# Strassen projection products: two blocks of 272 columns against one block of 512 with the samples' 64 columns beside them

## The chip, the cores and the metric

One core of a Trainium2 chip runs the whole kernel as a single program. The metric is the device time of one execution in microseconds, and the median over several executions is compared. TensorE (PE in the profile; its weight loads are shown as PEld) multiplies, VectorE (DVE), ScalarE (ACT) and GpSimd (POOL) do the elementwise work, and the queues of SyncE (SP) and ScalarE issue most transfers between the chip's memory and the core.

## The reference, cut to what matters

One layer of a hybrid decoder runs over a prompt of 1024 rows and over 8 samples of 8 rows, with all numbers in float32. After an RMSNorm and a modulation, one wide projection feeds everything else:

```
h = rmsnorm(x) * (1 + scale) + shift
[u_pool | z_pool | z_ssm | xBC | dt | g] = h @ w_in        # 1024 -> 8224 columns
p = (pool_mix(u_pool) * silu(z_pool)) @ w_pool_out
s = gated_rmsnorm(SSD(conv(xBC)) + D*x, z_ssm) @ w_ssm_out
x = x + gate * ((sigmoid(g_pool) * p + sigmoid(g_ssm) * s) @ w_o)
```

The outputs are the two normed results and the new pool, conv and SSM states of the prompt and of the samples. This case is about `h @ w_in`, and about the step that carries the samples' SSM states through their 8 rows.

## The kernel before, in words

The kernel keeps activations transposed: 128 channels lie on the partitions, and the T = 1088 columns are the 1024 prompt rows followed by the 64 sample rows. Every float32 operand of a large product is split into a high part (rounded to the fast float32r type) and a low part (the rest), and a product is the sum of three float32r products: high by high, high by low, low by high. In `product` these are three matmuls for each of four blocks of 128 channels, so 12 matmuls make one sum in a PSUM bank.

**The projection.** After `first` (start-up, norm, modulation, and two blocks of 128 output channels by plain products) 62 blocks of 128 output channels of `w_in` are left. They are made two at a time by `pair`, 31 pairs, each with the Strassen-Winograd scheme of seven products: the four 512x128 weight blocks b11, b12, b21, b22 of a pair are combined by `pair_w` (a few differences, then `split` into `whi` and `wlo` tiles by ACT and POOL), and the columns T are cut into a left and a right half of HF = 544 columns. `combine` makes the sums and differences of activation blocks once (lists S1, S2, S3, and the fourth in place in `hh_` and `hl_`). A product over 544 columns does not fit a PSUM bank of 512 float32 columns, so `product` runs it in two steps of SB = 272 columns, alternating between the three banks of pool `psA` (tiles named mm) and the five of `psB` (tiles named ps). After each step a DVE operation adds the bank to a running sum (`s1`, `u2`, `u3`, `c2`) or writes an output through the function `done` of the pair's two consumers. The samples' columns are the last 64 of the right half and go through the scheme with the rest.

**The order of the work.** `light` pairs (z and the gates) and `heavy` pairs (conv and pooling channels) are woven; `between` runs a step of a consumer's later work (conv taps, pooling) and a step of the next pair's weight preparation after each product. PE executes its instructions in the order in which the program gives them. Beside the last ten light pairs (`samples_beside`) run first the dt steps and then `ssd_samples(g)` for the four groups g: decays, the products inside the samples, and for each half of four samples the transposes of the old states (`h0_load`), a product with C, an outer product that renews the states, and the store. A fixed pace (`SSTEPS`) spreads those steps over the products.

**After the pairs.** The chunks of the prompt's SSD run beside the products with `w_pool_out` and `w_ssm_out` (`gemm_`), then come the last eight output products and `w_o`. The change does not touch that part.

Of the kernel before, what the change touches and what calls it, by code (L numbers as in the profile page):

```python
# [41 lines left out]
HF, SB = T // 2, T // 4  # L42
# [4 lines left out]
def tile_pool_ssd_step(  # L47
# [18 lines left out]
    psB = ctx.enter_context(tc.tile_pool(name="psB", bufs=5, space=PSUM))  # L66
# [32 lines left out]
    def PA():  # L99
        return psA.tile([P, 512], F32, tag="mm", name=nm("mm"))  # L100

# [163 lines left out]
    def ada_mm(part, k):  # L265
        a, b = PARTS[part]
        n = (b - a) * P // 2
        if k == 0:
            pm[part] = PB()
# [25 lines left out]

    hb = []

    def h_tile(k, j):
# [162 lines left out]

    S2, S1, S3 = [None] * 4, [None] * 4, [None] * 4

    def a_part(i, j):
        sl = lambda s: slice(HF * i + SB * s, HF * i + SB * s + SB)
        return lambda k, s: (hh_[4 * j + k][:, sl(s)], hl_[4 * j + k][:, sl(s)])

    def s_part(lst):
        return lambda k, s: (lst[k][:, 0, SB * s:SB * s + SB], lst[k][:, 1, SB * s:SB * s + SB])

    def s4_part(k, s):
        sl = slice(HF + SB * s, HF + SB * s + SB)
        return hh_[k][:, sl], hl_[k][:, sl]

    def combine():
        L_, R_ = slice(0, HF), slice(HF, T)

        big = []
# [5 lines left out]
        def room(lst, k):  # L484
            if lst is S1:
                lst[k] = (hs.tile([P, 2, HF], F32R, tag="sq", name="S1", bufs=1) if k == 3 else R((P, 2, HF), F32R))
            else:
                if k == 0:
                    big.append(Y4(hs).rearrange("p k (j n) -> p k j n", j=2))
                lst[k] = big[-1][:, k]  # L490
# [36 lines left out]
    def pair_w(c0, c1, pri, early):  # L527
        def run():
# [14 lines left out]
            def add(x):  # L543
                with tc.high_priority(pri):
                    w.append(split(x, highs, eng=V if early else None))
# [5 lines left out]
            def first_steps():  # L551
# [13 lines left out]
                diff(b12, b12, b11)  # L565
                add(b12)
                yield
                add(b22)
                yield

            def steps():
# [7 lines left out]
                diff(b12, b12, b11)  # L579
                add(b12)  # L580
                add(b21)
                diff(t2, t2, b21, eng=nc.gpsimd)
# [11 lines left out]
    turn = [0]  # L594

    def product(w, A, use):
        for s in range(2):
            turn[0] ^= 1
            p = (PA if turn[0] else PB)()[:, :SB]
            for k in range(4):  # L600
                hi, lo = w[0][:, k], w[1][:, k]
                ah, al = A(k, s)
                mm(p, hi, ah, start=(k == 0), stop=False)  # L603
                mm(p, hi, al, start=False, stop=False)  # L604
                mm(p, lo, ah, start=False, stop=(k == 3))  # L605
            with tc.high_priority(PRI):
                use(s, p)

    def strassen(w, d0, d1, early=False):
        def tmp(tag):  # L610
            return pa.tile([P, 2, SB], F32, tag=tag, name=nm(tag))

        def add(x, y):
            return lambda s, p: V.tensor_tensor(y[:, s], x[:, s], p, ALU.add)

        def out(d, o, x, buf, op=ALU.add):
            def use(s, p):
                def put(dst, a=0, b=SB, v=lambda t: t):
                    V.tensor_tensor(dst, v(x[:, s, a:b]), v(p[:, a:b]), op)
                d(o + SB * s, SB, put, buf)  # L620
            return use

        def fourth(s, p):
            out(d1, HF, u3, c2)(s, p)
            add(u2, u2)(s, p)
        s1, u2, u3, c2 = tmp("s1"), tmp("u2"), tmp("u3"), tmp("c2")
        if early:
            def fifth(s, p):
                out(d0, HF, s1, u3, ALU.subtract)(s, u3[:, s])
                out(d1, HF, s1, c2)(s, p)  # L630
                add(u2, u2)(s, p)
            product(w[0], a_part(0, 0), lambda s, p: act(s1[:, s], p, AF.Copy))
            yield
            product(w[1], a_part(0, 1), out(d0, 0, s1, c2))
            yield
            product(w[2], a_part(1, 1), lambda s, p: act(u3[:, s], p, AF.Copy))
# [7 lines left out]
            product(w[6], s4_part, out(d1, 0, u2, u2))  # L644
            return
        product(w[0], a_part(0, 0), lambda s, p: act(s1[:, s], p, AF.Copy))
# [62 lines left out]
    def to_dram(func, dst):  # L709
        yield  # L710

        def done(o, n, comb, buf):
            s = (o % HF) // SB
            comb(buf[:, s])
            act(buf[:, s], buf[:, s], func)
            if s:
                store_(dst[:, o + n - HF:o + n], buf.rearrange("p s n -> p (s n)"))
# [33 lines left out]
    def u_unit(gi):  # L751
# [9 lines left out]
        def done(o, n, comb, buf):  # L761
            e = min(o + n, SEQ) - o
            comb(up[:, 15 + o:15 + o + e], 0, e)
            if e < n:
                comb(us[:, :, 15:23], e, n, lambda t: t.rearrange("p (b t) -> p b t", t=8))
# [48 lines left out]
    def zp_unit(gi):  # L814
# [3 lines left out]
        def done(o, n, comb, buf):  # L818
            comb(sz[:, o:o + n])
# [15 lines left out]
    def gate_mm(k):  # L835
        if k == 0:
            gp2.append(PB())
# [187 lines left out]
    def conv_unit(mc, dst):  # L1025
# [10 lines left out]
        def done(o, n, comb, buf):  # L1036
            e = min(o + n, SEQ) - o
            comb(rp[:, 3 + o:3 + o + e], 0, e)
            if e < n:
                comb(seg[:, :, 3:11], e, n, lambda t: t.rearrange("p (b t) -> p b t", t=8))  # L1040
# [30 lines left out]
    def dt_end():  # L1071
# [11 lines left out]
        s1 = sp.tile([P, NS], F32, tag="bt", name="s1", bufs=2)  # L1083
# [93 lines left out]
    SSTEPS = 18  # L1177
# [39 lines left out]
    def ssd_samples(g):  # L1217
        S = NS
        xb = spt([P, 6, NS], "hst", 2)
        load(xb, xbc_d[g][:, :, SEQ:])  # L1220
        Bf, Cf = xb[:, 4], xb[:, 5]
        E2 = spt([P, 4, NS], "hst", 2)
        load_E(E2, g)
        dec = spt([P, 8, P], "dec", 2)[:NS, :, :NS]
        decays(dec, g, NC)
        far(dec, NC)
        exps(dec, g, NC)
        h0s = {}

        def h0_load(j):  # L1230
            hf, q = divmod(j, 4)
            h0 = spt([P, 4, P], "h0", H0B)
            load(h0, state_ssm[0, 4 * hf:4 * hf + 4, 8 * g + 2 * q:8 * g + 2 * q + 2].rearrange("b h p n -> (h p) b n"))
            h0s[j] = h0
        h0_load(0)
        yield
        px = PB()
        for q in range(4):
            nc.tensor.transpose(px[:S, q * P:(q + 1) * P], xb[:, q], ident)
        pc = PB()  # L1240
        mm(pc[:S, :S], Bf, Cf, start=True, stop=True)
        xd = spt([P, 8, 64], "xd", 2)
        V.tensor_tensor(xd[:S], px[:S].rearrange("p (h d) -> p h d", d=64),
                        dtT[:S, NC, 8 * g:8 * g + 8].unsqueeze(2).to_broadcast([S, 8, 64]), ALU.mult)
        V.tensor_tensor(dec, dec, pc[:S, :S].unsqueeze(1).to_broadcast([S, 8, S]), ALU.mult)
        for j in range(1, H0B - 1):
            h0_load(j)
        yield
        t = spt([P, 4, P], "xd", 2)[:, :, :NS]
        for q in range(4):  # L1250
            act(t[:, q], xb[:, q], AF.Copy, scale=Dv[:, 4 * g + q:4 * g + q + 1])
        yield
        V.tensor_tensor(t, inner(xd, dec, S), t, ALU.add)
        for hf in range(2):
            rep = spt([P, 5, 2, 3, 16], "yt", 1).rearrange("p q a r i -> p q (a r i)").rearrange(
                "p q (r i) -> p q r i", i=32)
            nc.gpsimd.tensor_copy(rep, xb[:, 0:5, 32 * hf:32 * hf + 32].unsqueeze(2).to_broadcast([P, 5, 3, 32]))
            px = PB()
# [7 lines left out]
            xh = spt([P, 512], "dec", 2, F32R)  # L1266
# [3 lines left out]
            bx = spt([P, P], "bt", 2, F32R)  # L1270
            act(bx[:96], pb[:96, :P], AF.Copy)
            V.tensor_tensor(bx[32:64], pb[32:64, :P], bx[32:64].bitcast(F32), ALU.subtract)
            Bb = spt([P, 4, P], "dec", 2, F32R)
            V.tensor_tensor(Bb[:96], bx[:96].bitcast(F32).unsqueeze(1).to_broadcast([96, 4, P]),
                            blk3.unsqueeze(2).to_broadcast([96, 4, P]), ALU.mult)
            cz = spt([P, 4, 32], "cz", 2)
            V.memset(cz, 0.0)
            V.tensor_copy(cz[:, :, 0:8], Cf[:, 32 * hf:32 * hf + 32].rearrange("p (b i) -> p b i", i=8))
            yield
            po = None  # L1280
            hts = {}
            for q in range(5):
                if q < 4:
                    j = 4 * hf + q
                    if j + H0B - 1 < 8:
                        h0_load(j + H0B - 1)
                    pt = PB()
                    for b in range(4):
                        nc.tensor.transpose(pt[:, b * P:(b + 1) * P], h0s[j][:, b, :], ident)
                    hts[q] = spt([P, 512], ("hT", "yt")[q % 2], 1)  # L1290
                    act(hts[q], pt, AF.Copy)
                if q > 0:
                    r = q - 1
                    h0 = h0s.pop(4 * hf + r)
                    if po is None:
                        po = PB()
                    for b in range(4):
                        mm(po[32 * b:32 * b + 32, r * P:(r + 1) * P], cz[:, b, :], hts[r][:, b * P:(b + 1) * P],
# [637 lines left out]
```

## Time and profile before

| | |
|---|---|
| median of 3 runs | 1298.07 us (1294.51 to 1299.71) |
| the profiled execution's own time | 1298.25 us |
| its span, first to last instruction | 1296.5 us |
| granted TensorE clock over the span | 0.996 |
| busy: PE, PEld | 1261.6 us (97%), 1168.5 us (90%) |
| busy: DVE, ACT, POOL | 887.8 us, 696.2 us, 675.4 us |
| matmuls, weight loads | 9739, 9739 |
| HBM read, written | 167.06 MB, 83.01 MB |

The span is 1.75 us shorter than the time of the same execution. A matmul's duration in the profile runs from its start to its last result, and matmuls overlap in the pipeline, so the distance between the starts of neighbours, not the duration, says what one costs. A name such as `mm<-Y,whi` reads: tile mm is written from tiles Y and whi; the shape `128*128 128x272` is the weights, then the moving columns. Every matmul has a weight load of its own, also where two neighbours use the same weights.

### The profile page before, as it was taken

Reading aid. Unit: us, or ns where it says so; the run is one execution under the profiler, and the core shown is the slowest. Engines: PE = TensorE matmul, PEld = TensorE weight load, DVE = VectorE, ACT = ScalarE, POOL = GpSimd, SP = SyncE. Lnnn points to the kernel's source line nnn. Section 1 sums busy time; section 2 is a strip of 40 time slices with the busy share of each in tenths; the row PEclk is TensorE's granted clock in tenths of the full one; section 3 lists DMA queues with packets and bytes.
Section 4 is the critical chain, followed back from the end, with each engine's and each line's share of the span. In section 5 each row is a group of like instructions: output and inputs, shape, how many; then the busy total and the mean of one; then the engine's idle time right before and its main releaser. Section 6 shows DMA issues by size and latency. Waiting matters only on the chain. (4 is left out here: it accounts for less than half of the span.)

```text
span 1296.5 us, 26406 instructions
## 1 busy us (share of the span) xinstructions
PE 1261.6 (97%) x9739; PEld 1168.5 (90%) x9739; DVE 887.8 (68%) x1512; ACT 696.2 (54%) x1656; POOL 675.4 (52%) x563
## 2 busy tenths in 40 slices
PE   7999999999999999999999999999999999999998
PEld 6779999989999999998889999888888888999786
DVE  4685778866978678775767665477565878476433
ACT  5664356375656564545455464676887766201111
POOL 1007668677869776664344453366676656214000
PEclk9999999999999999999999999999999999999999
DMA  9837345465455544444556455999988665475631
GB/s 331 255 110 232 109 157 174 136 212 162 153 183 198 157 159 129 159 135 128 160 154 194 148 170 174 346 358 364 312 282 277 203 204 163 170 268 160 228 105 50
DMA packets 233793, 251.68 MB, mean 194 GB/s; under 512 B 31265, under 2 KB 177905, under 8 KB 233658
## 3 DMA queue, kind: packets, MB, share of 16 engines
q1 hardware_dynamic: 161568, 171.60, 41.7%
q10 hardware_dynamic: 72098, 78.41, 17.6%
q8 instruction: 77, 1.26, 0.4%
q14 instruction: 50, 0.41, 0.1%
HBM read 167.06 MB, written 83.01 MB: 193 GB/s over the span
## 5 line engine op out<-in xcount | busy, mean ns | idle before, releaser
L163 POOL TENSOR_TENSOR wlo<-rawA,whi 128x512 fp32r<-128x512 f32 x120 | 185.3, 1549 | 188.1 <-ACT whi L160 101.7
L163 POOL TENSOR_TENSOR wlo<-raw,whi 128x512 fp32r<-128x512 f32 x92 | 151.1, 1650 | 121.9 <-ACT whi L160 112.8
L354 PE MATMUL mm<-Y,whi 128*128 128x352 f32 (+1 forms) x480 | 163.3, 340 | 0.9 <-DVE G L1785 0.7
L355 PE MATMUL mm<-Y,whi 128*128 128x352 f32 (+1 forms) x480 | 157.4, 328 | 1.0 <-DVE Y L1459 1.0
L356 PE MATMUL mm<-Y,wlo 128*128 128x352 f32 (+1 forms) x480 | 156.8, 327 | 0.0
L605 PE MATMUL mm<-Y,wlo 128*128 128x272 f32 x496 | 143.6, 290 | 4.5 <-POOL wlo L163 4.1
L603 PE MATMUL mm<-Y,whi 128*128 128x272 f32 x496 | 146.4, 295 | 0.2
L603 PE MATMUL ps<-Y,whi 128*128 128x272 f32 x496 | 144.4, 291 | 1.4 <-ACT o L803 1.4
L604 PE MATMUL ps<-Y,whi 128*128 128x272 f32 x496 | 143.1, 289 | 0.0
L604 PE MATMUL mm<-Y,whi 128*128 128x272 f32 x496 | 142.9, 288 | 0.0
L605 PE MATMUL ps<-Y,wlo 128*128 128x272 f32 x496 | 142.6, 288 | 0.0
L160 ACT ACTIVATE whi<-rawA 128x512 fp32r<-128x512 f32 x125 | 78.1, 626 | 97.0 <-PE ps L604 43.2
L1051 DVE SCALAR_TENSOR_TENSOR GA<-GA,cvT,GA 128x1112 f32<-128x1112 f32 x72 | 126.7, 1763 | 0.6 <-ACT GA L1048 0.5
L160 ACT ACTIVATE whi<-raw 128x512 fp32r<-128x512 f32 x96 | 58.7, 626 | 91.2 <-DVE raw L549 43.0
L605 PEld LDWEIGHTS mm<-Y,wlo 128*128 128x128 f32 x496 | 93.4, 188 | 6.4 <-POOL wlo L163 5.4
L354 PEld LDWEIGHTS mm<-Y,whi 128*128 128x128 f32 x480 | 90.2, 188 | 6.9 <-issue 4.3
L603 PEld LDWEIGHTS ps<-Y,whi 128*128 128x128 f32 x496 | 93.3, 188 | 2.7 <-ACT o L803 1.6
L603 PEld LDWEIGHTS mm<-Y,whi 128*128 128x128 f32 x496 | 93.3, 188 | 2.3 <-issue 0.8
L604 PEld LDWEIGHTS mm<-Y,whi 128*128 128x128 f32 x496 | 93.4, 188 | 0.7 <-issue 0.6
L604 PEld LDWEIGHTS ps<-Y,whi 128*128 128x128 f32 x496 | 93.3, 188 | 0.3 <-issue 0.2
L605 PEld LDWEIGHTS ps<-Y,wlo 128*128 128x128 f32 x496 | 93.4, 188 | 0.2 <-issue 0.2
L1196 ACT ACTIVATE dec<-dec,acT 128x128 f32<-128x128 f32 (+1 forms) x288 | 86.7, 383 | 10.0 <-POOL dec L1187 6.3
(445 smaller groups left out, 3790.3 us busy)
## 6 DMA issues: line engine op xcount, KB each, us to landing
rawA<-in_w_in SPq DMA_DIRECT2D x46, 512.0 KB
dec<-acs_d SPq DMA_DIRECT2D x32, 512.0 KB
xbc<-GA ACTq DMA_DIRECT2D x24, 512.0 KB
xb<-xbc SPq DMA_DIRECT2D x32, 384.0 KB
rawA<-in_w_in SPq DMA_DIRECT2D x32, 256.0 KB
pw<-in_w_ssm_out ACTq DMA_DIRECT2D x32, 256.0 KB
ws<-ph ACTq DMA_DIRECT2D x32, 256.0 KB
ws<-pw SPq DMA_DIRECT2D x32, 256.0 KB
```

What stands on the lines that cost most here:

```text
L160: ins = act(hi[:, :, :ncols], raw[:, :, :ncols], AF.Copy)
L163: (eng or nc.gpsimd).tensor_tensor(lo[:, :, :ncols], raw[:, :, :ncols], hi[:, :, :ncols].bitcast(F32), ALU.subtract)
L354: mm(ps[:, :n], a, rh[k][:, o:o + n], start=(k == 0), stop=False)
L355: mm(ps[:, :n], a, rl[k][:, o:o + n], start=False, stop=False)
L356: mm(ps[:, :n], b, rh[k][:, o:o + n], start=False, stop=(k == nk - 1))
L603: mm(p, hi, ah, start=(k == 0), stop=False)
L604: mm(p, hi, al, start=False, stop=False)
L605: mm(p, lo, ah, start=False, stop=(k == 3))
L1051: V.scalar_tensor_tensor(d[:, :n], rp[:, k:k + n], cvT[:, 24 * k + mc:24 * k + mc + 1], d[:, :n], ALU.mult, ALU.add)
L1196: act(dec[:, h], dec[:, h], AF.Exp, bias=acT[:S, c, 8 * g + h:8 * g + h + 1], scale=-1.0)
```

## The change: what it does

The halves are halves of the prompt alone, HF = 512 columns, and each of the seven products is one run of 12 matmuls of 512 columns into one bank of `psA`. The samples' 64 columns are left out of the scheme and multiplied plainly by the four weight blocks in `sample`: with the first 512 input channels, a high-weight matmul takes the high and the low activations side by side (128 columns, for which `h_tile` lays them at one stride) and a low-weight matmul takes the high ones (64 columns); with the other 512 input channels, three matmuls of 64 columns. That is 8 + 12 matmuls for each output block. Both output blocks' sums lie in one bank of a new one-bank pool `psC` (`psB` has four banks in place of five), and one `tensor_reduce` per output block adds the two parts. The plain product needs b12 itself, so a pair has eight `split`s, not seven; the extra low part is made on DVE, and the difference b12 - b11 is written over b11. The consumers' `done` functions take the prompt's columns as 512 wide and the samples' in a call of its own; for z and the gates that is one more store.

`ssd_samples` becomes a class `Samples`: `before` (decays, inner products' operands and the first half's `prepare`) of the next group runs during steps 8 to 10 of this group, the second half's `prepare` runs within the first half, and a group takes 13 steps; `SSTEPS` is 14, not 18. Some tiles get tags of their own (`rep`, `E2`).

```diff
-HF, SB = T // 2, T // 4
+HF = SEQ // 2
...
-    psB = ctx.enter_context(tc.tile_pool(name="psB", bufs=5, space=PSUM))
+    psB = ctx.enter_context(tc.tile_pool(name="psB", bufs=4, space=PSUM))
+    psC = ctx.enter_context(tc.tile_pool(name="psC", bufs=1, space=PSUM))
...
+            for r in range(4):
+                hsm[r] = hb[r // 2][:, r % 2 * 2:r % 2 * 2 + 2, SEQ:]
-        return hb[j][:, k] if k < 4 else G((P, T), F32R)
+        return hb[k // 2][:, k % 2 * 2 + j] if k < 4 else G((P, T), F32R)
...
-                diff(b12, b12, b11)
-                add(b12)
+                diff(b11, b12, b11)
+                add(b11)
                 add(b21)
+                add(b12, None, V)
...
     def product(w, A, use):
-        for s in range(2):
-            turn[0] ^= 1
-            p = (PA if turn[0] else PB)()[:, :SB]
-            for k in range(4):
-                hi, lo = w[0][:, k], w[1][:, k]
-                ah, al = A(k, s)
-                mm(p, hi, ah, start=(k == 0), stop=False)
-                mm(p, hi, al, start=False, stop=False)
-                mm(p, lo, ah, start=False, stop=(k == 3))
-            with tc.high_priority(PRI):
-                use(s, p)
+        p = PA()
+        for k in range(4):
+            hi, lo = w[0][:, k], w[1][:, k]
+            ah, al = A(k)
+            mm(p, hi, ah, start=(k == 0), stop=False)
+            mm(p, hi, al, start=False, stop=False)
+            mm(p, lo, ah, start=False, stop=(k == 3))
+        with tc.high_priority(PRI):
+            use(p)
...
+        def sample(w, t, j, d=None):
+
+            if not banks:
+                banks.append(PC())
+            ps = banks[0][:, P * t:P * t + P]
+            for k in range(4):
+                a, b = w[0][:, k], w[1][:, k]
+                if j == 0:
+                    mm(ps.rearrange("p (j n) -> p j n", j=2), a, hsm[k], start=(k == 0), stop=False)
+                    mm(ps[:, :NS], b, hsm[k][:, 0], start=False, stop=False)
+                else:
+                    hi, lo = hh_[4 + k][:, SEQ:], hl_[4 + k][:, SEQ:]
+                    mm(ps[:, :NS], a, hi, start=False, stop=False)
+                    mm(ps[:, NS:], a, lo, start=False, stop=False)
+                    mm(ps[:, :NS], b, hi, start=False, stop=(k == 3))
+            if d is not None:
+                with tc.high_priority(PRI):
+                    d(SEQ, NS, lambda dst: V.tensor_reduce(dst, ps.rearrange("p (j b i) -> p b i j", j=2, i=8),
+                                                           axis=mybir.AxisListType.X, op=ALU.add), None)
+        banks = []
...
-        product(w[0], a_part(0, 0), lambda s, p: act(s1[:, s], p, AF.Copy))
+        product(w[0], a_part(0, 0), lambda p: act(s1, p, AF.Copy))
+        sample(w[0], 0, 0)
         yield
         product(w[1], s_part(S2), add(s1, u2))
...
         product(w[4], a_part(0, 1), out(d0, 0, s1, s1))
+        sample(w[4], 0, 1, d0)
+        sample(w[5], 1, 0)
         yield
-        product(w[5], a_part(1, 1), out(d0, HF, u3, u3, ALU.subtract))
+        product(w[6], a_part(1, 1), out(d0, HF, u3, u3, ALU.subtract))
         yield
-        product(w[6], s4_part, out(d1, 0, u2, u2))
+        product(w[7], s4_part, out(d1, 0, u2, u2))
+        sample(w[7], 1, 1, d1)
...
-    SSTEPS = 18
+    SSTEPS = 14
...
+    def all_samples():
+        groups = [Samples(g) for g in range(NG)]
+        groups[0].h0_load(0)
+        yield from groups[0].before()
+        for s_, n_ in zip(groups, groups[1:] + [None]):
+            ahead = n_.before() if n_ else iter(())
+            for i, _ in enumerate(s_.steps()):
+                if i in (8, 9, 10):
+                    next(ahead, None)
+                    if i == 9 and n_:
+                        n_.h0_load(0)
+                yield
```

More of the change, by code (lines that the diff above doesn't have):

```diff
@@ L268, in ada_mm @@
         if k == 0:
-            pm[part] = PB()
+            pm[part] = PC()
         for j in range(4):
@@ L296, in tile_pool_ssd_step @@
     hb = []
+    hsm = [None] * 4
     def h_tile(k, j):
@@ L613, in add, with use @@
         def add(x, y):
-            return lambda s, p: V.tensor_tensor(y[:, s], x[:, s], p, ALU.add)
+            return lambda p: V.tensor_tensor(y, x, p, ALU.add)
         def out(d, o, x, buf, op=ALU.add):
[L617 to L620, printed above, removed]
-            return use
-        def fourth(s, p):
-            out(d1, HF, u3, c2)(s, p)
-            add(u2, u2)(s, p)
+            def use(p):
+                d(o, HF, lambda dst: V.tensor_tensor(dst, x, p, op), buf)
@@ new lines, in out, with fourth @@
+            return use
+        def fourth(p):
+            out(d1, HF, u3, c2)(p)
+            add(u2, u2)(p)
+        def sample(w, t, j, d=None):
[16 more added lines that the diff above has]
+                                                           axis=mybir.AxisListType.X, op=ALU.add), None)
@@ L1215, in spt, with __init__, h0_load @@
         return sp.tile(list(shape), dt, tag=tag, name=nm(tag), bufs=bufs)
[L1217 to L1230, printed above, removed]
+    class Samples:
+        def __init__(self, g):
+            self.g, self.h0, self.half = g, {}, {}
+        def h0_load(self, j):
@@ L1231, in h0_load @@
             hf, q = divmod(j, 4)
-            h0 = spt([P, 4, P], "h0", H0B)
+            g = self.g
+            self.h0[j] = h0 = spt([P, 4, P], "h0", H0B)
             load(h0, state_ssm[0, 4 * hf:4 * hf + 4, 8 * g + 2 * q:8 * g + 2 * q + 2].rearrange("b h p n -> (h p) b n"))
[L1234 to L1251, printed above, removed]
@@ new lines, in before @@
+        def before(self):
+            g, S = self.g, NS
+            self.xb = xb = spt([P, 6, NS], "hst", 2)
+            load(xb, xbc_d[g][:, :, SEQ:])
+            Bf, Cf = xb[:, 4], xb[:, 5]
+            self.dec = dec = spt([P, 8, P], "dec", 2)[:NS, :, :NS]
+            decays(dec, g, NC)
+            far(dec, NC)
+            exps(dec, g, NC)
+            yield
+            px = PB()
+            for q in range(4):
+                nc.tensor.transpose(px[:S, q * P:(q + 1) * P], xb[:, q], ident)
+            pc = PB()
+            mm(pc[:S, :S], Bf, Cf, start=True, stop=True)
+            self.xd = xd = spt([P, 8, 64], "xd", 2)
+            V.tensor_tensor(xd[:S], px[:S].rearrange("p (h d) -> p h d", d=64),
+                            dtT[:S, NC, 8 * g:8 * g + 8].unsqueeze(2).to_broadcast([S, 8, 64]), ALU.mult)
+            V.tensor_tensor(dec, dec, pc[:S, :S].unsqueeze(1).to_broadcast([S, 8, S]), ALU.mult)
+            it = self.prepare(0)
+            next(it)
+            yield
+            next(it)
+            yield
@@ new lines, in steps @@
+        def steps(self):
+            g, S, xb, h0s = self.g, NS, self.xb, self.h0
+            E2 = spt([P, 4, NS], "E2", 1)
+            load_E(E2, g)
+            for j in range(g > 0, H0B - 1):
+                self.h0_load(j)
+            t = spt([P, 4, P], "xd", 2)[:, :, :NS]
+            for q in range(4):
+                act(t[:, q], xb[:, q], AF.Copy, scale=Dv[:, 4 * g + q:4 * g + q + 1])
+            V.tensor_tensor(t, inner(self.xd, self.dec, S), t, ALU.add)
+            yield
+            second = self.prepare(1)
+            for hf in range(2):
+                xh, Bb, cz = self.half[hf]
+                po = None
+                hts = {}
+                for q in range(5):
+                    if q < 4:
+                        j = 4 * hf + q
+                        if j + H0B - 1 < 8:
+                            self.h0_load(j + H0B - 1)
+                        pt = PB()
+                        for b in range(4):
+                            nc.tensor.transpose(pt[:, b * P:(b + 1) * P], h0s[j][:, b, :], ident)
+                        hts[q] = spt([P, 512], ("hT", "yt")[q % 2], 1)
+                        act(hts[q], pt, AF.Copy)
+                    if q > 0:
+                        r = q - 1
+                        h0 = h0s.pop(4 * hf + r)
+                        if po is None:
+                            po = PB()
+                        for b in range(4):
+                            mm(po[32 * b:32 * b + 32, r * P:(r + 1) * P], cz[:, b, :], hts[r][:, b * P:(b + 1) * P],
+                               start=True, stop=True)
+                        pu = PB()
+                        mm(pu, xh[:96, r * P:(r + 1) * P], Bb[:96].rearrange("p b n -> p (b n)"), start=True, stop=True)
+                        for b in range(4):
+                            cc_ = 32 * hf + 8 * b + 7
+                            V.scalar_tensor_tensor(h0[:, b, :], h0[:, b, :], E2[:, r, cc_:cc_ + 1],
+                                                   pu[:, b * P:(b + 1) * P], ALU.mult, ALU.add)
+                        store_(new_ssm_s[0, 4 * hf:4 * hf + 4, 8 * g + 2 * r:8 * g + 2 * r + 2]
+                               .rearrange("b h p n -> (h p) b n"), h0)
+                    if q in (1, 3) and hf == 0:
+                        next(second)
+                    if q < 4:
+                        yield
+                yo = spt([P, 512], "hT", 1)
+                act(yo, po, AF.Copy)
+                yield
+                pn = PB()
+                for q in range(4):
+                    nc.tensor.transpose(pn[:, q * P:(q + 1) * P], yo[:, q * P:(q + 1) * P], ident)
+                tn = spt([P, 4, P], "yt", 1)[:, :, :32]
+                V.tensor_tensor(tn.rearrange("p q (b i) -> p q b i", i=8),
+                                pn.rearrange("p (q b i) -> p q b i", q=4, i=32)[:, :, :, 0:8],
+                                E2[:, :, 32 * hf:32 * hf + 32].rearrange("p q (b i) -> p q b i", i=8), ALU.mult)
+                th = t[:, :, 32 * hf:32 * hf + 32]
+                V.tensor_tensor(th, th, tn, ALU.add)
+                if hf == 0:
@@ L1534, in tile_pool_ssd_step @@
     run_units(units, 1, lambda: next(pre, None))
-    side = iter([it for g in range(NG) for it in [ssd_samples(g)] * SSTEPS])
+    side = all_samples()
     due, made_ = [0.0], [0]
@@ L1568, in samples_beside @@
                 to_chunks()
-            next(next(side, iter(())), None)
+            next(side, None)
     SPARE = 7
@@ L1584, in tile_pool_ssd_step @@
     run_units(light[-LAST:], 1, samples_beside)
-    for it in side:
-        next(it, None)
+    for _ in side:
+        pass
     if not seq:
```

146 lines of the change are left out of this document (56 added, 90 removed).

## The prediction

> **What bounds the kernel now.** I read the page's busy time and slices first, then the stages, then the starts of single matmuls.
>
> ```profile
> span 1296.5 us, 26406 instructions
> PE 1261.6 (97%) x9739; PEld 1168.5 (90%) x9739; DVE 887.8 (68%) x1512; ACT 696.2 (54%) x1656; POOL 675.4 (52%) x563
> PE   7999999999999999999999999999999999999998
> DVE  4685778866978678775767665477565878476433
> ```
>
> TensorE is busy 97% of the span and in nearly every fortieth of it; no other engine is near. Busy alone says little, since a matmul's duration covers its pipeline. The stages (cut where the first and last Strassen product stand, where the dt steps begin and where the samples' steps begin) say how much of that is idle:
>
> ```profile
> core 0: us, PE busy (x) PEld busy (x) DVE busy (x) ACT busy (x) POOL busy (x), PEclk, DMA share, GB/s
> 79.30:560.00 480.70, 474.05 (x3711) 465.15 (x3710) 367.58 (x566) 268.55 (x633) 346.89 (x219) 1.00 0.50 162
> 560.00:613.00 53.00, 50.55 (x394) 48.77 (x394) 37.04 (x68) 27.47 (x58) 25.23 (x19) 1.00 0.39 115
> 613.00:825.10 212.10, 209.82 (x1798) 194.50 (x1797) 134.59 (x324) 108.44 (x229) 93.11 (x72) 0.98 0.59 178
> 825.10:1200.00 374.90, 369.39 (x2779) 334.62 (x2778) 258.45 (x375) 228.59 (x616) 203.27 (x219) 1.00 0.77 256
> ```
>
> The change lies in the first three rows, 745.8 us, of which TensorE idles 6.65 + 2.45 + 2.28 = 11.4 us. So there the time is TensorE's queue, and a change is worth what it makes of the sum of distances between the starts of matmuls.
>
> **How many matmuls.** The first of the three lines of `product`, counted over that stretch:
>
> ```profile
> core 0: us, PE busy (x) PEld busy (x), PEclk, DMA share, GB/s
> 79.30:825.10 745.80, 506.83 (x1736) 327.13 (x1736) 1.00 0.52 163
> ```
>
> Each of the three lines has as many: 5208 matmuls of 272 columns, 168 for each of 31 pairs (7 products, 2 steps, 12 matmuls). By the code after, a pair has 7 x 12 = 84 of 512 columns and, for the samples, 2 x (8 + 12) = 40 thin ones, 8 of 128 and 32 of 64 columns; the built program's order of instructions holds 2604 and 1240 of them, 31 times these. In streamed columns almost nothing changes: 168 x 272 = 45,696 before, 84 x 512 + 8 x 128 + 32 x 64 = 46,080 after. All depends on what a matmul costs beside its columns.
>
> **What one costs.** Starts in the timeline of TensorE. Between the first two rows lie 33 more of 272 columns, so 34 distances; between 1250.89 and 1255.98 lie 22 distances of 512 columns (the output products at the end, same float32r kind, 128x128 weights); between 1249.76 and 1250.89 lie 5; between the last two 10 of 256 columns.
>
> ```profile
> 419.72 0.29 PE L605 MATMUL ps<-Y,wlo 128*128 128x272 f32 x1
> ...
> 423.95 0.29 PE L603 MATMUL mm<-S,whi 128*128 128x272 f32 x1
> ...
> 1249.76 0.39 PE L1883 MATMUL ps<-Y,G 128*128 128x512 f32 x1
> ...
> 1250.89 0.39 PE L1882 MATMUL ps<-Y,m 128*128 128x512 f32 x1
> ...
> 1255.98 0.39 PE L1883 MATMUL ps<-Y 128*128 128x512 f32 x1
> ...
> 1285.78 0.28 PE L1884 MATMUL ps<-m,G 128*128 128x256 f32 x1
> ...
> 1286.98 0.28 PE L1882 MATMUL ps<-Y,m 128*128 128x256 f32 x1
> ```
>
> 272 columns: 4.23 us / 34 = 124.4 ns. 512 columns: 5.09 / 22 = 231.4 ns (226 in the five before). 256 columns: 120 ns. Per column these are 0.457, 0.452 and 0.469 ns: a wide matmul pays its columns and next to no fixed price. So merging two steps of 272 into one of 512 saves only the columns that it leaves out.
>
> **A thin one.** The trace has no thin float32r product. The nearest row streams one column against 128x128 weights:
>
> ```profile
> 1137.95 2.12 PEld L1730 LDWEIGHTS ps<-ones,sq_acc 128*128 128x128 f32 x18
> 1138.11 2.05 PE L1730 MATMUL ps<-ones,sq_acc 128*128 128x1 f32 x18
> 1140.08 0.44 PE L354 MATMUL mm<-Y,whi 128*128 128x384 f32 x1
> 1207.55 0.30 PEld L1764 LDWEIGHTS ps<-Y,sh 128*128 128x128 f32 x2 [0.37 <-DMA Y<-wo]
> 1207.89 0.19 PEld L1883 LDWEIGHTS ps<-Y,G 128*128 128x128 f32 x1
> ```
>
> Eighteen matmuls of one column take 1140.08 - 1138.11 = 1.97 us, 109.4 ns each: nothing is left to stream, so this is the distance between weight loads. It is plain float32; the fourth row shows the same for float32r weights: two loads in 0.30 us, each lasting 0.19 like the one below it, so 0.11 us apart. A matmul of 272 columns (124.4 ns) just hides the next load, one of 64 (64 x 0.452 = 29 ns) does not. The Trainium skill, TensorE: Matmul & The Clock Gate, section LDWEIGHTS, has P / 1.2 for P weight columns, 107 ns for 128, which speaks against this change; by it the sum below would be 3 us less. Break-even for the change is (168 x 124.4 - 84 x 231.4) / 40 = 36.5 ns for a thin matmul; the rows say three times that.
>
> **The sum.** Per pair, before: 168 x 124.4 = 20.90 us. After: 84 x 231.4 = 19.44 us, 40 x 109.4 = 4.38 us, together 23.81 us. Difference 2.91 us, times 31 pairs: +90.3 us. All of it lies on the path, as TensorE runs in order and has no idle time to take it. Bounds: 512 columns at 226 and a load at 108 ns give 2.41 us, +75 us; 512 at 235 (0.46 ns a column) and a thin matmul at the 120 ns of 256 columns give 3.64 us, +113 us.
>
> **What I cost at nothing, with its cover.**
>
> ```profile
> L614 DVE TENSOR_TENSOR u<-u,ps 128x272 f32<-128x272 f32 x61 | 26.3, 431 | 16.3 <-PE ps L605 16.2
> L1436 DVE TENSOR_TENSOR v<-ps,xD 128x512 f32<-128x512 f32 x32 | 21.9, 684 | 5.6 <-PE ps L1211 5.1 <-PE ps L1208 0.4
> L163 DVE TENSOR_TENSOR wlo<-rawA,whi 128x512 fp32r<-128x512 f32 x5 | 3.3, 683 | 0.7 <-ACT whi L160 0.7
> L1104 DVE TENSOR_REDUCE xd<-ps 128x32 f32<-128x128 f32 x1 | 0.3, 277 | 0.0
> L1051 DVE SCALAR_TENSOR_TENSOR GA<-GA,cvT,GA 128x1112 f32<-128x1112 f32 x72 | 126.7, 1763 | 0.6 <-ACT GA L1048 0.5
> L160 ACT ACTIVATE whi<-rawA 128x512 fp32r<-128x512 f32 x125 | 78.1, 626 | 97.0 <-PE ps L604 43.2
> ```
>
> VectorE for a pair: before, 14 additions of 272 columns from PSUM, 14 x 0.431 = 6.0 us; after, 7 of 512, 7 x 0.684 = 4.8 us, two reductions, 2 x 0.277, and the low part of b12, 0.683 us: 6.0 us again. ScalarE gets one more split, 0.63 us, and a thin store and activation per gate block; it has 404 of 746 us filled. All hide under TensorE's longer pair; uncovered, the split would cost 31 x (0.63 + 0.68) = 41 us, but it is asked for four products ahead. If anything, slower pairs give the others more air: the 11.4 us of idle could shrink, which I keep for the low end (1361) and not for the sum.
>
> The samples' steps keep their matmuls, transposes, state loads and stores. They are moved: `before` puts the next group's loads on SP, its exponentials on ScalarE and its masks on POOL ahead of this group's last steps, and the E2 load behind them on SP, where state and weight loads queue after it. What that could win is bounded by TensorE's idle in that stage, 212.10 - 209.82 = 2.3 us; a lost cover there costs about as little, since TensorE has the products to run. I take zero.
>
> New waits: products use three banks, not eight. The fourth product needs the first's bank, two products later, 2 x 2.78 = 5.6 us; one 512-wide addition is 0.68 us, and three conv taps of 1.76 us would have to stand ahead of it. The samples' single bank is written again one product, 2.8 us, after the pair's last reduction is asked for. Behind such a wait everything on TensorE queues. Zero in the sum, a rival below.
>
> The profiled execution took 1298.25 us, 0.2 us over the median of 1298.07, so the sum goes on the median: 1298 + 90 = **1388 us**.
>
> **The rivals.**
>
> *Thin matmuls cost their columns (0.07).* If the loads of a run of thin matmuls ran ahead under the 512-wide ones, 32 would cost 28.9 and 8 would cost 57.8 ns, 1.39 us; it decides below 36.5 ns a piece. The pair is then 20.83 us, -0.07: 1296 us; with 226 ns for 512 columns -0.53 us a pair, 1282 us. Against it: the loads of one column stand 109 ns apart with nothing to hinder them. For it: none of them stood behind a wide product. I halve the chance between faster and within 0.5% (6.5 us, about what a measurement of this kernel can tell from no change). The same page, section Back-to-back issue gap, has about 25 ns for 1 to 64 columns; the trace's 109.4 ns disagrees.
>
> *Half hidden (0.07).* A load runs while the thin matmul before it streams, so 109.4 - 28.9 = 80.5 ns for 64 columns and 51.6 for 128: 2.99 us, +1.53 us a pair, 1345 us. Against: the 256-column row leaves room for such an overlap but the one-column row cannot show it. That section gives about 81 ns as the sustained distance at 128 columns, by which all 40 would make +55 us.
>
> *Thin float32r at plain float32's pace (0.10).*
>
> ```profile
> 839.90 1.10 PE L1424 MATMUL ps<-xw,bt 128*128 128x512 f32 x2
> L1424 PE MATMUL ps<-xw,bt 128*128 128x512 f32 x64 | 32.8, 594 | 1.3 <-ACT hst L1428 1.3
> ```
>
> A plain float32 product of 512 columns is two instructions, the second starting 1.10 - 0.59 = 0.51 us after the first, so about 1.02 us or 2 ns a column. If thin float32r fell to that, 8 x 0.255 + 32 x 0.128 = 6.1 us: +4.7 us a pair, 1443 us. Nothing in the trace shows float32r under 256 columns, and at 256 there is no sign of it.
>
> *Banks (0.06).* VectorE is 7 to 9 tenths busy in the heavy pairs. If TensorE waits for one conv tap, 1.76 us, in each of 16 heavy pairs, that is 28 us on top: 1416 us.
>
> **How the numbers follow.** The forecast has 0.70, at 1361 to 1411 by its own bounds. The range is 1343 to 1430: it takes in the forecast, the half-hidden load and the banks, 0.83, and leaves out the first and third rival. Slower: 0.70 + 0.07 + 0.10 + 0.06 = 0.93; faster 0.035, same 0.035, rounded to 0.04 and 0.03.
>
> **What would show it.** In the profile after: 9739 falls by 31 x 44 = 1364 matmuls; the Strassen stage grows from 746 to about 836 us; thin starts stand 108 to 112 ns apart, 512-wide ones 226 to 235; weight loads of a thin run follow each other without a gap; the stretch from 825.10 to the end of the span keeps its 471 us; TensorE's waits stay near 11 us. Thin starts under 40 ns apart, or 512-wide ones under 197 ((168 x 124.4 - 40 x 109.4) / 84, where the sum is zero), would make the forecast wrong; TensorE waiting for DVE on tile mm or pc would show the banks.

## The result, and the profile after

The kernel after takes 1377.05 us (median of 4 runs, 1374.63 to 1378.49) against 1298.89 us for the kernel before in the same comparison: 1.0584 times as long, 95% interval 1.0559 to 1.0610. The forecast was 1388 us in a range of 1343 to 1430; the chance given to "slower" was 0.93. The profiled execution's span is 1376.8 us, 80.3 us over that of before.

The page of the kernel after, the same lines:

```profile
span 1376.8 us, 23473 instructions
PE 1344.0 (98%) x8375; PEld 1140.0 (83%) x8375; DVE 904.3 (66%) x1360; ACT 712.5 (52%) x1623; POOL 660.1 (48%) x563
PE   7999999999999999999999999999998999999998
DVE  4684778775968487776566666367664777559433
```

There are 1364 matmuls fewer, and TensorE is the limit even more than before. The stages of the kernel after, with the boundary again where the first `gemm_` product starts:

```profile
core 0: us, PE busy (x) PEld busy (x) DVE busy (x) ACT busy (x) POOL busy (x), PEclk, DMA share, GB/s
80.70:894.00 813.30, 811.87 (x4535) 675.61 (x4535) 550.66 (x806) 423.77 (x893) 454.22 (x310) 1.00 0.48 150
894.00:1376.80 482.80, 463.17 (x3188) 409.99 (x3187) 304.12 (x435) 242.20 (x647) 201.04 (x221) 0.99 0.68 225
```

The pairs take 813.3 us in place of 745.8: 67.5 of the 80.3 us. The stretch behind them takes 482.8 in place of 471.4: 11.4 us. The start-up gives 1.4 us. The stretch behind the pairs varies by several us from one execution to another (6 us, in the experiments), so its 11.4 us are known no better. TensorE's idle time among the pairs has fallen from 11.4 to 813.30 - 811.87 = 1.4 us.

One pair with no matmuls but its own shows the mechanism. The sixteenth begins and ends, in the timeline of TensorE of the kernel before, at

```profile
413.71 0.39 PE L603 MATMUL mm<-Y,whi 128*128 128x272 f32 x1
434.82 0.29 PE L603 MATMUL mm<-Y,whi 128*128 128x272 f32 x1
```

and in that of the kernel after at

```profile
450.63 0.50 PE L610 MATMUL mm<-Y,whi 128*128 128x512 f32 x1
...
456.45 0.39 PE L610 MATMUL mm<-Y,whi 128*128 128x512 f32 x1
...
459.20 0.39 PE L610 MATMUL mm<-Y,whi 128*128 128x512 f32 x1
...
474.37 0.48 PE L610 MATMUL mm<-Y,whi 128*128 128x512 f32 x1
```

So 21.11 us became 23.74 us, +2.63 us. Between 456.45 and 459.20 stand one whole product's 12 matmuls, 2.75 us or 229 ns each; 84 of these make 19.25 us, and the 40 thin ones have the other 4.49 us, 112 ns each. The weight loads of a run of eight thin matmuls, with the wide ones around them, say why (timeline of PEld, kernel after; start and duration):

```profile
371.91 0.19 PEld L640 LDWEIGHTS pc<-Y,whi 128*128 128x128 f32 x1
372.14 0.19 PEld L641 LDWEIGHTS pc<-Y,wlo 128*128 128x128 f32 x1
372.25 0.19 PEld L640 LDWEIGHTS pc<-Y,whi 128*128 128x128 f32 x1
372.36 0.19 PEld L641 LDWEIGHTS pc<-Y,wlo 128*128 128x128 f32 x1
...
372.92 0.19 PEld L610 LDWEIGHTS mm<-Y,whi 128*128 128x128 f32 x1
373.03 0.19 PEld L611 LDWEIGHTS mm<-Y,whi 128*128 128x128 f32 x1
373.27 0.19 PEld L612 LDWEIGHTS mm<-Y,wlo 128*128 128x128 f32 x1
...
374.84 0.19 PEld L646 LDWEIGHTS pc<-G,wlo 128*128 128x128 f32 x1
374.95 0.11 PEld L1096 LDWEIGHTS ps<-ident,t 128*27 128x27 f32 x1
374.98 0.15 PEld L803 LDWEIGHTS ps<-ident,stp 120*128 120x128 f32 x1
```

In the thin run a load starts every 0.11 us, one behind the other, whether the matmul that it serves streams 64 or 128 columns; only the first is hidden behind a wide matmul, and the first wide one after the run waits for its load too. Between wide matmuls loads stand 0.23 us apart: there the matmul sets the distance. The last three rows, from the end of the next thin run, argue that the slot belongs to the load and its size, and is not a fixed price of any instruction: after a load of 128 weight columns the next one starts 0.11 us later, after a load of 27 weight columns 0.03 us later. No experiment changed the size of the weights, so this stays argued.

### The profile page after: what moved, and what is told of

Read it like the earlier page. It is cut to its first block, busy times and chain, and to the rows that moved or that the text cites. A ratio compares the mean times of both kernels' runs of the same rounds, so it can differ in the third digit from the quotient of the medians.

```text
span 1376.8 us, 23473 instructions
## 1 busy us (share of the span) xinstructions
PE 1344.0 (98%) x8375; PEld 1140.0 (83%) x8375; DVE 904.3 (66%) x1360; ACT 712.5 (52%) x1623; POOL 660.1 (48%) x563
## 4 chain that ended last, share of the span: by engine, by line
PE 82%; DMA 5%; DVE 3%; ACT 3%; POOL 2%; issue 2%; SPq 0%; ACTq 0%; POOLq 0%; DVEq 0%
PE mm L610 14%; PE mm L612 13%; PE mm L611 13%; PE mm L363 5%; PE mm L364 4%; PE mm L365 4%; PE ps L1954 2%; PE ps L1955 2%; PE pc L640 2%; PE ps L1956 2%; PE pc L645 2%; PE ps L1243 2%; PE pc L646 2%; PE ps L232 2%; PE pc L644 2%
## 5 line engine op out<-in xcount | busy, mean ns | idle before, releaser
L167 POOL TENSOR_TENSOR wlo<-rawA,whi 128x512 fp32r<-128x512 f32 x120 | 176.8, 1475 | 266.3 <-ACT whi L164 180.9
L167 POOL TENSOR_TENSOR wlo<-raw,whi 128x512 fp32r<-128x512 f32 x92 | 147.3, 1603 | 119.5 <-ACT whi L164 118.5
L610 PE MATMUL mm<-Y,whi 128*128 128x512 f32 x496 | 202.0, 408 | 0.0
L612 PE MATMUL mm<-Y,wlo 128*128 128x512 f32 x496 | 196.4, 397 | 1.4 <-POOL wlo L167 1.3
L611 PE MATMUL mm<-Y,whi 128*128 128x512 f32 x496 | 195.6, 395 | 0.0
L164 ACT ACTIVATE whi<-rawA 128x512 fp32r<-128x512 f32 x156 | 97.3, 627 | 118.3 <-PE mm L611 38.3
L612 PEld LDWEIGHTS mm<-Y,wlo 128*128 128x128 f32 x496 | 93.3, 188 | 22.8 <-POOL wlo L167 2.6
L610 PEld LDWEIGHTS mm<-Y,whi 128*128 128x128 f32 x496 | 93.5, 189 | 18.2 <-issue 0.8
L611 PEld LDWEIGHTS mm<-Y,whi 128*128 128x128 f32 x496 | 93.5, 189 | 18.1 <-issue 0.6
L610 PE MATMUL mm<-G,whi 128*128 128x512 f32 x248 | 100.6, 406 | 0.0
L363 PEld LDWEIGHTS mm<-Y,whi 128*128 128x128 f32 x480 | 91.1, 190 | 8.5 <-issue 4.1
L611 PE MATMUL mm<-G,whi 128*128 128x512 f32 x248 | 97.5, 393 | 0.0
L612 PE MATMUL mm<-G,wlo 128*128 128x512 f32 x248 | 97.3, 392 | 0.0
L364 PEld LDWEIGHTS mm<-Y,whi 128*128 128x128 f32 x480 | 91.3, 190 | 1.4 <-DVE Y L1531 1.3
L365 PEld LDWEIGHTS mm<-Y,wlo 128*128 128x128 f32 x480 | 91.2, 190 | 0.2
L441 POOL TENSOR_TENSOR pw<-pw,ph 128x512 fp32r<-128x512 f32 x40 | 66.2, 1656 | 15.3 <-ACT ph L439 15.2
```

The source lines that it names most:

```text
L164: ins = act(hi[:, :, :ncols], raw[:, :, :ncols], AF.Copy)
L167: (eng or nc.gpsimd).tensor_tensor(lo[:, :, :ncols], raw[:, :, :ncols], hi[:, :, :ncols].bitcast(F32), ALU.subtract)
L363: mm(ps[:, :n], a, rh[k][:, o:o + n], start=(k == 0), stop=False)
L364: mm(ps[:, :n], a, rl[k][:, o:o + n], start=False, stop=False)
L365: mm(ps[:, :n], b, rh[k][:, o:o + n], start=False, stop=(k == nk - 1))
L441: nc.gpsimd.tensor_tensor(raw.bitcast(F32R), raw, hi.bitcast(F32), ALU.subtract)
```

## The experiments

Two theories of the thin matmuls stood against each other: that each costs the distance of a weight load, or that it costs its columns. And two of the rest: that making the samples' steps ahead won time, or that the longer pairs did.

**Twice the columns, as many matmuls** (`thin_wider`).

```diff
-                hsm[r] = hb[r // 2][:, r % 2 * 2:r % 2 * 2 + 2, SEQ:]
+                hsm[r] = hb[r // 2][:, r % 2 * 2:r % 2 * 2 + 2, SEQ - NS:]
...
-                    mm(ps[:, :NS], b, hsm[k][:, 0], start=False, stop=False)
+                    mm(ps[:, 0].rearrange("p h n -> p (h n)"), b, hh_[k][:, SEQ - NS:], start=False, stop=False)
...
-                    hi, lo = hh_[4 + k][:, SEQ:], hl_[4 + k][:, SEQ:]
+                    hi, lo = hh_[4 + k][:, SEQ - NS:], hl_[4 + k][:, SEQ - NS:]
```

> The kernel after, with every thin matmul given twice the columns it needs: the 64-column ones stream 128, the 128-column ones 256; the sums that are used stay the same and the number of matmuls too. If a thin matmul costs the distance between weight loads (about 109 ns), the widening is free except for 8 a pair that now stream 256 columns (118 to 120 ns): 8 x 31 x 10 ns = 2.5 us, so 1377 to 1382 us. If it costs its columns, a pair pays 32 x 28.9 + 8 x 57.8 ns = 1.39 us more, 43 us in all: about 1420 us.

Measured: 1375.36 us (1.0593, 1.0559 to 1.0627), where the kernel after has 1.0584. The same pair in its timeline:

```profile
451.44 0.50 PE L610 MATMUL mm<-Y,whi 128*128 128x512 f32 x1
475.28 0.45 PE L610 MATMUL mm<-Y,whi 128*128 128x512 f32 x1
```

23.84 us against 23.74. Doubling the streamed columns of 40 matmuls costs 0.1 us a pair where the columns theory asks for 1.39, and the total did not rise, where it asks for 43 us: it falls.

**Nearly no thin matmuls** (`thin_left_out`), one for each output block.

```diff
-            for k in range(4):
-                ...
+            if j == 0:
+                mm(ps.rearrange("p (j n) -> p j n", j=2), w[0][:, 0], hsm[0], start=True, stop=True)
```

> The kernel after, with 38 of the 40 thin matmuls of each pair left out (one is left for each output block, so that its bank is written); the samples' results lack those terms. The built matmuls fall by 1178. By the load floor at 103 to 109 ns each that is 121 to 128 us less: about 1250 to 1256 us, up to 14 us more if TensorE then waits for others as it did before. If thin matmuls cost their columns: 31 x (32 x 28.9 + 6 x 57.8) ns = 39 us less, about 1338 us.

Measured: 1313.01 us, 1.0113 times before (1.0061 to 1.0164): 64 us less than the kernel after, half of what the load floor alone foretold. By the total the run would not decide, since 64 lies between the 39 us of the columns theory and the 121 to 128 of the load floor. Where a pair is bound by TensorE the price is right: the eleventh pair, in this kernel and in the kernel after,

```profile
305.10 0.39 PE L610 MATMUL mm<-Y,whi 128*128 128x512 f32 x1
324.72 0.39 PE L610 MATMUL mm<-Y,whi 128*128 128x512 f32 x1
```

```profile
327.06 0.50 PE L610 MATMUL mm<-Y,whi 128*128 128x512 f32 x1
351.04 0.47 PE L610 MATMUL mm<-Y,whi 128*128 128x512 f32 x1
```

takes 19.62 us in place of 23.98, 4.36 us for 38 matmuls, 115 ns each; by their columns (32 x 28.9 + 6 x 57.8 ns) they would cost 1.27 us. Elsewhere something else is late. The waits of TensorE in this kernel (us in total, times, longest) and its stages:

```profile
PE mm L363 <- DMA whi<-wp: 16.8, 1, 16.8
PE mm L610 <- DVE GA L625: 8.8, 4, 3.5
PE mm L612 <- POOL wlo L167: 6.7, 8, 1.7
```

```profile
80.50:827.80 747.30, 698.08 (x3358) 546.13 (x3357) 563.89 (x807) 421.73 (x901) 457.02 (x310) 0.98 0.52 164
```

TensorE idles 747.3 - 698.1 = 49 us up to the next stage: it waits for VectorE's outputs in the conv pairs, for the low weight halves from POOL, and 16.8 us for the first weights of the next stage. So the columns rival was wrong in both experiments. Even with its thin matmuls almost gone the wide scheme is no faster than the narrow one, since other engines then set the pace of many pairs and of the step to the next stage.

**Every thin matmul twice** (`thin_twice`; the samples' projections come out doubled).

```diff
-            for k in range(4):
+            for k, c in ((k, c) for k in range(4) for c in (0, 1)):
```

> The kernel after with every thin matmul made twice into the same sum, 1240 more in all (the samples' projections come out doubled). TensorE is then longer busy than any other engine, so nothing else should set the pace. By the load floor at 103 to 109 ns each: 128 to 135 us more, 1505 to 1512 us. If a thin matmul cost its columns (1.39 us a pair): 43 us more, 1420 us.

Measured: 1525.18 us, 148 us more for 1240 matmuls, 119 ns each, and 13 us above the top of what was expected. The granted clock over the span is 0.985 in both of its runs and 0.996 in the profiled run of the kernel after; by these, (0.996 - 0.985) x 1523 = 17 us of the 148 are an estimate of what the clock took. Why it was lower is not shown. The sixteenth pair is 28.20 us long, 4.46 more than in the kernel after, 111.5 ns for each of 40:

```profile
527.53 0.50 PE L610 MATMUL mm<-Y,whi 128*128 128x512 f32 x1
555.73 0.48 PE L610 MATMUL mm<-Y,whi 128*128 128x512 f32 x1
```

With left out, doubled and widened together, the price of a thin matmul is shown: 112 to 115 ns in quiet pairs, whether it streams 64 or 128 columns.

**Two steps of 256** (`two_steps_256`): the merging undone, with the samples still beside.

```diff
-        for k in range(4):
+        for s in (slice(0, HF // 2), slice(HF // 2, HF)):
+            for k in range(4):
+                ...
+                mm(p[:, s], hi, ah[:, s], start=(k == 0), stop=False)
```

> The kernel after with each product of 512 columns run as two steps of 256 into the two halves of its bank, one addition after both. If a wide matmul costs its columns and little else, by the rows 2 x 120 - 231.4 = 8.6 ns for each of 2604: 22 us more, about 1399 us. If the merging itself saved a large fixed price per matmul, much more than that; if TensorE did not set the pace, no change, 1377 us.

Measured: 1398.07 us (1.0761, 1.0729 to 1.0793), 21 us over the kernel after. The sixteenth pair is 24.28 us, 0.54 more than with 512 columns:

```profile
460.64 0.39 PE L611 MATMUL mm<-Y,whi 128*128 128x256 f32 x1
484.92 0.36 PE L611 MATMUL mm<-Y,whi 128*128 128x256 f32 x1
```

Halving the number of wide matmuls is worth 0.54 us in this pair, 6 ns for each matmul saved. That is the gain of merging, and the thin matmuls cost eight times as much. Over the kernel the 21 us are 8 ns for each, as expected, but not all of it is the matmuls': among the pairs

```profile
81.40:917.30 835.90, 827.85 (x7139) 805.54 (x7138) 541.01 (x805) 419.39 (x888) 457.24 (x310) 1.00 0.47 146
```

TensorE idles 8 us, against 1.4 in the kernel after.

**The other part of the change alone** (`ahead_only`), in the narrow kernel: class `Samples` and `SSTEPS = 14`, with `blkS` and `A` moved into other tiles' buffers to make room.

> The kernel before with the second part of the change alone: samples' steps made ahead, 13 steps a group, the pace for 14; products stay two steps of 272 columns. Two small tiles share buffers so that it fits. If the lost time in the samples' stage (pairs 23 to 29 took 6.7 us less in the kernel after than 2.63 us a pair more would make them) went through this part: about 1291 us. If it went only because longer pairs give the other engines more time: 1298 us, no change.

Measured: 1301.19 us, 1.0021 (1.0001 to 1.0041): nothing gained, 0.2% lost, or 0.4% at most by the interval. The theory that this part won the lost time falls for the narrow kernel.

**The first part alone** (`wide_only`): the kernel after with `ssd_samples` and `SSTEPS = 18` put back.

> The kernel after with the first part of the change alone: 512-column products and thin matmuls, but the samples' steps as they were before. If making them ahead is what won time in the samples' stage: about 1384 us. If the longer pairs won it: 1377 us, as the kernel after.

Measured: 1391.57 us (1.0716, 1.0687 to 1.0744), 14.5 us over the kernel after, and not for the reason that I gave. The seven pairs beside the samples take 216 us, less than the 222 of the kernel after, but they hold fewer of the other matmuls, 516 against 589; then TensorE waits, by its waits in this kernel:

```profile
PE mm L363 <- DMA whi<-wp: 15.3, 1, 15.3
```

The samples' last step stands behind the last product here, and the loads of the next stage queue on SP behind loads that wait themselves, for the stores of states and for a store of the last pairs. The waits of SP from 850 to 912 us:

```profile
SPq L1268 <- DMA out<-h: 22.6, 4, 16.9
SPq L1432 <- DMA gs<-c: 11.8, 1, 11.8
```

So the steps made ahead are worth 14 us in the wide kernel and nothing in the narrow one.

**A sooner pace** (`wide_only_sooner`), `SPARE = 14` in place of 7.

> wide_only with the samples' steps paced to end 14 products before the last and not 7 (SPARE 14). In wide_only the last step stood behind the last product, and TensorE then waited 15.3 us for the first weights of the next stage. If the lateness is only the pace: the wait goes and about 1376 us remain, as the kernel after. If the steps themselves can't go faster (their state loads and stores set the end): 1391 us as wide_only, or a wait elsewhere in its place.

Measured: 1391.81 us (1.0715, 1.0680 to 1.0751), no change. In the two traces every engine executes the same instructions in the same order, and the pairs beside the samples take the same times to a few hundredths of a us. The edit left the order as it was, so this run repeats `wide_only` and does not test the pace. The wait is 15.6 us, put down here to an operand that ScalarE makes from another load of the next stage. What the repeat does show is how far one and the same order varies: the stretch behind the pairs in `wide_only` and here

```profile
910.80:1385.50 474.70, 461.67 (x3186) 408.03 (x3186) 308.12 (x434) 237.05 (x635) 204.20 (x222) 0.99 0.67 227
913.90:1394.60 480.70, 465.01 (x3186) 410.44 (x3186) 305.93 (x434) 237.43 (x635) 204.14 (x222) 0.99 0.67 224
```

differs by 6 us. The waits of SP from 650 us on, for the state loads, in this run and in the kernel after:

```profile
SPq L1268 <- DMA out<-h: 145.7, 27, 19.4
SPq L1262 <- DMA out<-h: 131.0, 27, 17.0
```

In both, twenty-seven state loads wait for the store that empties their buffer, 146 and 131 us in all, so these waits alone do not tell the late kernel from the other. Why this chain ends in time in the narrow kernel and in the kernel after, and late in `wide_only`, is not settled.

**One bank fewer in the narrow kernel** (`narrow_4banks`, and `ahead_4banks` with the steps made ahead): `psB` with four banks, the fifth unused.

> The kernel before with four banks in place of five in psB, the fifth left unused. wide_only was 14 us slower than the kernel after, while ahead_only gained nothing. If the old order of samples' steps suffers from the bank that psC takes: some 10 to 15 us slower than before, 1308 to 1313 us. If it suffers from the wide products themselves: 1298 us, no change.

> The kernel ahead_only with four banks in place of five in psB. If samples' steps made ahead are what lets four banks do: as ahead_only, 1301 us, whatever narrow_4banks gives. If fewer banks cost the same in both orders: as much slower as narrow_4banks is.

Measured: 1310.21 us, 1.0085 (1.0062 to 1.0107), and 1313.44 us, 1.0102 (1.0076 to 1.0128). The bank is worth about 10 us in either order; the steps made ahead do not make up for it. Where it goes in the profile of narrow_4banks:

```profile
79.90:828.80 748.90, 735.37 (x5899) 706.70 (x5899) 537.01 (x958) 409.79 (x923) 465.18 (x310) 1.00 0.52 163
828.80:1308.30 479.50, 462.81 (x3188) 409.23 (x3186) 302.67 (x435) 243.98 (x652) 202.02 (x221) 0.99 0.67 226
```

3.1 us more among the pairs, and 8.1 behind them (471.4 before). But `ahead_only`, with five banks, has 478.6 us behind its pairs, so a single profile does not place the loss.

**The bank given back** (`bank_back`): after the pairs, every fifth bank asked of `psB` is `psC`'s.

```diff
+        if turn_[0] is not None:
+            turn_[0] += 1
+            if turn_[0] % 5 == 0:
+                return psC.tile([P, 512], F32, tag="pc", name=nm("ps"))
```

> The kernel after, but once the pairs are done every fifth bank that the later stages ask of psB is psC's, so that they turn over five banks again. In the profile the stretch behind the pairs took 11 us more in the kernel after than in the one before, and narrow_4banks cost 9 us. If that is the bank: 1366 to 1369 us, the stretch back at 472 to 475 us. If it is something else that the wide kernel leaves behind: 1377 us.

Measured: 1374.59 us (1.0579, 1.0550 to 1.0609), 2.5 us under the kernel after and inside its interval. The stretch behind the pairs:

```profile
895.20:1373.30 478.10, 460.18 (x3188) 408.78 (x3187) 297.58 (x435) 241.94 (x647) 203.28 (x221) 0.99 0.67 227
```

4.7 of the 11.4 us came back in this profile, less than the 6 us by which two profiles of one order differ, and the time stayed above the 1366 to 1369 us expected if the bank was the cause. In seven of the eight profiles of kernels with the steps made ahead TensorE waits 4.5 to 7.8 us (2.8 in ahead_4banks) for VectorE's state of the last chunk of a group, as in the kernel after:

```profile
PE ps L1513 <- DVE hst L1504: 6.5, 2, 5.6
```

while the kernel before has 1.7 us there, wide_only 1.5 and wide_only_sooner 2.4. Bank and wait would together make up some 9 of the 11 us, but each stands on single profiles, so the cause of these 11 us stays open.

## Why the prediction was right

**The floor of a thin matmul** held: 109.4 ns from matmuls of one column became 112. The rivals by which thin matmuls cost their columns, or had their loads half hidden, were both wrong, and so was the one of plain float32's pace: at 2 ns a column, twice the columns for the 32 of 64 would have cost 4.1 us more a pair, and the widening cost 0.1. The Trainium skill, TensorE: Matmul & The Clock Gate, section LDWEIGHTS, gives P / 1.2 ns for the load of P columns, by which 107 ns is the estimate for 128, and this trace agrees nearly (loads 0.11 us apart). The 25 ns for 1 to 64 columns and the 81 ns at 128 in the section Back-to-back issue gap of the Trainium skill's same page are not what this case shows, 112 ns.

The trace of the kernel before had a row that spoke against half-hidden loads and that the prediction did not use, four transposes (not float32r products) of 128 columns against 128x128 weights:

```profile
637.58 0.60 PE L1289 MATMUL ps<-ident,h 128*128 128x128 f32 x4
```

One lasts 0.28 us, so their starts stand (0.60 - 0.28) / 3 = 0.11 us apart; that rival would have had 0.05.

**The wide matmul** was taken at 231.4 ns and is 229; the pair after, 23.81 us, is 23.74.

**The pair before** was the mis-sized term: 34 distances of a quiet stretch gave 124.4 ns and 20.90 us, while a whole quiet pair is 21.11 us, 125.7 ns. That is the larger part of why the difference was forecast as 2.91 us and is 2.63, 81.5 us for 31 pairs in place of 90.3.

**The air.** The 11.4 us of idle time, which I had kept for the low end, did shrink, to 1.4. That is 10 of the 14 us between 81.5 and the measured 67.5; where the other 4 went is not traced.

**What I costed at nothing.** VectorE and the extra split were covered, and none of TensorE's waits of 0.3 us or more in the kernel after is for VectorE in a product of the pairs or a thin matmul, so the rival of the banks did not come either. That "the stretch from 825.10 to the end of the span keeps its 471 us" was wrong, by 11 us in this profile. I counted `psB`'s lost bank for the products alone and not for the stages behind them. It is worth about 10 us in the narrow kernel by narrow_4banks; that it is the cause in the wide one bank_back does not show. The two misses, 23 us less from the pairs and 11 more from the end, cancel by half, so that the total came closer than its terms is partly luck.

**The samples' steps made ahead** were taken at zero. In the narrow kernel that is what they bring; in the wide one they keep 14 us off, which a bound from TensorE's idle time in the old kernel could not show, as the wait that they avoid did not exist there.

**The rival of columns** needed a thin matmul under 36.5 ns, or under (21.11 - 19.25) / 40 = 46.5 ns by the measured pairs; one costs 112. Its 1282 to 1296 us are doubtful even so: thin_left_out has what is late next, and ends at 1313.

## What to carry to other kernels

Before a product is cut into a wide and a thin part, compare the distance between starts of the thin part with that of two weight loads: here every 128x128 load takes a slot of 0.11 us, and at the 0.457 ns a column of the 272-column matmuls that is as long as some 240 columns (an estimate), so a matmul of fewer pays for columns that it doesn't have. Two steps of 272 columns already hide their loads, and merging has little left to save: from 256 to 512 columns it was 6 ns a matmul. When a stage's work is taken off the bound engine, ask what is late next in each stage, and count a bank that is moved in every stage that uses its pool.

## What the runs showed of the hardware

Widening 40 thin float32r matmuls a pair from 64 or 128 columns to 128 or 256 cost 0.1 us a pair, 2.5 ns each; so float32r matmuls of 64 and 128 columns cost the same, with no sign of a slower form for few columns. In a thin run of the kernel after the loads start 0.11 us apart (0.11 or 0.12 by the rows).
